# A down projection in Winograd form on one Trainium2 core: the residual added by an accumulating transfer, and quarter sums of w2 kept in device memory

## The chip, the cores and the metric

The kernel runs on one core of one Trainium2 chip. A core has TensorE (PE, matrix products), VectorE (DVE), ScalarE (ACT), GpSimd (POOL) and SyncE (SP, which only issues transfers here). Transfers are issued from the queues of SP, ACT and POOL, and all of them are carried by the core's 16 DMA engines. Times are device microseconds (us) of one execution; the metric is their median over several executions, and lower is better.

## The reference, cut to what matters

One encoder layer is computed for a prompt of 2048 tokens and a sample of 256 tokens, with 1024 channels. The change touches only the end of the layer:

```python
h = rmsnorm(x, norm2_g[i]) * (1.0 + scale2) + shift2          # x is x1, the sum after the mixer
x = x + gate2 * (jnp.square(jax.nn.relu(h @ mlp_w1[i])) @ mlp_w2[i])
...
return rmsnorm(x, final_g)
```

`mlp_w2` is 4096 x 1024. Everything is float32, and a float32 product is made of three products of split operands (high by high, high by low, low by high).

## The kernel before, in words

The last part of the kernel is the down projection (`h @ mlp_w2`, the gate, the residual x1 and the final norm). The 18 token tiles of 128 tokens stand in nine pairs (`PAIRS`); `acc[2*i]` and `acc[2*i+1]` are the two tiles of pair i, each 128 x 1024, and stay in SBUF from the first addition to the output. The 4096 hidden channels are cut into four groups (g = 0 to 3). Each group is a 2 x 2 block product in Winograd form: seven products per pair, numbered o = 1 to 7, each of 12 matmuls of 128 x 512. The left operands come from device memory (`AD`, loaded into `araw`) and are split into high and low parts (`aop`: an ACT cast and a DVE subtraction, line 778). The right operands are quarters of w2, or sums of quarters, loaded by SP into `w2raw` (six buffers, half a quarter of 512 KB each), summed on DVE (lines 1107 and 1109) and split into `w2op` (three buffers).

A group is walked in sweeps over the pairs: (1, 6, 7), (2), (5, 3), (4) for groups 0 to 2, and (2), (1, 6, 7), (5, 3, 4) for group 3. Within a sweep the products are staggered: at step i come the first product of pair i, the second of pair i - 1 and the third of pair i - 2. A sweep of three has 27 products, 324 matmuls. Products of one pair in a sweep can share a PSUM bank and go on accumulating in it, so the second may start only when DVE has added the first into `acc` (line 1202).

The right operands are w2 quarters named by two digits: o = 5 needs 01 - 00, o = 6 needs 11 - (01 - 00), and o = 4 needs 10 - (11 - (01 - 00)). Each of the three starts again from the quarters: `w2_load` fetches two, three and four of them, for each of two halves h.

In group 3, `res(i, h)` applies the gate and adds x1 as soon as a tile has its first five terms, in the sweep (1, 6, 7): POOL multiplies `acc` by the gate `g2` (line 1159), adds `xe` (line 1160, x1 loaded from `X1` into three buffers) and issues the next load of x1 (`res_load`, line 1151). In the last sweep (5, 3, 4) each product is multiplied by the gate into `tm` and added (`last_add`, lines 1174 and 1175), ACT takes the sums of squares, and `out` applies the norm and stores the tile: for eight prompt tiles by ACT and a POOL multiplication (lines 1188 and 1189), for the other ten by one DVE operation (line 1191).

The program is written in the order of the loops; a planner then orders the instructions of each engine by its own estimates of their costs, and each engine and each queue runs its own in that order.

Of the kernel before, what the change touches and what calls it, by code (L numbers as in the profile page):

```python
# [9 lines left out]
F32 = mybir.dt.float32  # L10
# [3 lines left out]
ALU = mybir.AluOpType  # L14
# [4 lines left out]
P = 128  # L19
D = 1024  # L20
KT = 8
T = 16
# [8 lines left out]
PAIRS = ((0, 1), (2, 3), (4, 5), (6, 7), (8, 16), (9, 17), (10, 11), (12, 13), (14, 15))  # L31
# [105 lines left out]
def body(ctx, tc, I, O):  # L137
    nc = tc.nc
    v = nc.vector
    dram = ctx.enter_context(tc.tile_pool(name="dr", bufs=1, space=DRAM))  # L140
# [7 lines left out]
    def ps():  # L148
        return psp[0].tile([P, 512], F32, name="ps", tag="ps")
# [6 lines left out]
    X1 = dram.tile([NTILE, P, D], F32, name="X1")  # L156
    HOP = [dram.tile([3, P, 7, 4, P], F32, name=f"HOP{b}") for b in range(3)]
    WS = dram.tile([16, P, 4, 4, P], F32, name="WS")
    AD = [[dram.tile([P, 7, 4, 384], F32, name=f"AD{g}_{b}") for b in range(3)] for g in range(4)]

    R = "right"
# [267 lines left out]
    for part, (pw, tc_, tb_, t16) in enumerate(((PR, ARc, ARb, AR16), (PI, AIc, AIb, AI16))):  # L429
        for k0 in (0, 4, 8):  # L430
            n = 4 if k0 < 8 else 2
# [94 lines left out]
    for t0 in range(0, T, 4):  # L526
        dg_ = dgn
        for k in range(KT):
# [5 lines left out]
            for _ in range(SQ[t0 // 4] if k >= 4 else 0):  # L534
                t = next(ts, None)
# [22 lines left out]
    for g in range(0, 16, 2):  # L558
        pq = ps()
        for i in range(2):  # L560
            for m in range(2):
                x = 2 * i + m
# [149 lines left out]
    for b4 in range(16):  # L712
        u = load_u(l2, b4, 3)
        for q in range(4):
# [3 lines left out]
            for m in range(2):  # L718
                o = py[:, m * NCH:(m + 1) * NCH]
# [8 lines left out]
    for k in range(KT):  # L728
        for hb in range(2):
# [5 lines left out]
            for q in range(4):  # L735
                g = 4 * b4 + q
                py = ps()
                hf, hb_ = Hs[:, g, :], Hs[:, 64 + g, ::-1]
                for m, (of, ob) in enumerate(((0, 0), (128, 128))):
                    o = py[:, m * NCH:(m + 1) * NCH]  # L740
# [33 lines left out]
    def split(hi, lo, src, chain=False):  # L774
        with ExitStack() as st:
            for x in last if chain else ():
                st.enter_context(tc.issue_after(x.ins))
            ins = (nc.scalar.copy(hi, src), v.tensor_tensor(lo, src, hi.bitcast(F32), op=ALU.subtract))  # L778
        if chain:
            last[:] = ins  # L780
        return ins
# [134 lines left out]
    t = GORD[-1]  # L916
# [26 lines left out]
    def w_ops(b, i):  # L943
        ws = WS[i].rearrange("p o k c -> p (o k) c")
        one, two, both = slice(0, 1), slice(1, 2), slice(0, 2)
        ca, cb = (slice(256 * i + P * x, 256 * i + P * x + P) for x in range(2))
        if b == 0:
            ra, rb = w_raw((both, w1v[:, :, ca])), w_raw((both, w1v[:, :, cb]))
            yield w_split(ra)
            s = w_raw()  # L950
            v.tensor_tensor(s[:, 1], rb[:, 0], rb[:, 1], op=ALU.add)
            v.tensor_tensor(s[:, 0], s[:, 1], ra[:, 0], op=ALU.subtract)
            nc.gpsimd.dma_start(ws[:, 0:8], s.rearrange("p o k c -> p (o k) c"))
            yield w_split(s)
            v.tensor_tensor(rb[:, 0], ra[:, 0], rb[:, 0], op=ALU.subtract)
            v.tensor_tensor(ra[:, 1], ra[:, 1], s[:, 0], op=ALU.subtract)
            nc.gpsimd.dma_start(ws[:, 8:12], rb[:, 0])
            nc.gpsimd.dma_start(ws[:, 12:16], ra[:, 1])
            yield w_split(rb)
            yield w_split(ra[:, two])  # L960
        else:
            yield w_split(w_raw((both, w1v[:, :, ca])))
            yield w_split(w_raw((both, ws[:, 0:8])))
            yield w_split(w_raw((one, ws[:, 8:12]), (two, w1v[:, 4:8, cb])))
            yield w_split(w_raw((one, ws[:, 12:16]))[:, one])
# [12 lines left out]
    def product(bank, lhs, rhs, start):  # L978
        for k in range(4):
            for x, (a, b) in enumerate(((0, 0), (0, 1), (1, 0))):  # L980
                nc.tensor.matmul(bank, lhsT=lhs(a, k), rhs=rhs(b, k), start=start and k == 0 and x == 0,  # L981
                                 stop=k == 3 and x == 2, skip_group_check=True)

    def up_group(b, pairs, hops, load=None):
# [45 lines left out]
        for y in ys:  # L1030
# [10 lines left out]
            i = pairs[y]  # L1041
            nc.gpsimd.dma_start(AD[i // 4][b][:, :, i % 4], c[:, 0:7])  # L1042

# [39 lines left out]
    w2v = I["mlp_w2"].rearrange("o (g k a p) (d m) -> (o g) a d p k m", g=4, k=4, a=2, d=2)  # L1083
# [3 lines left out]

    def w2_load(g, o):

        need = {1: ("00",), 2: ("10",), 3: ("11",), 7: ("01", "11"), 5: ("01", "00"), 6: ("01", "00", "11"),  # L1090
                4: ("01", "00", "11", "10")}[o]
        for h in range(2):
            parts = []
            for a, d in need:
                x = dn.tile([P, 2, 512], F32, name="w2raw", bufs=6)
                nc.sync.dma_start(x, w2v[g, int(a), int(d), :, 2 * h:2 * h + 2])
                parts.append(x)
            yield parts

    def w2_op(g, o, loads=None):  # L1100
        op = None
        for h, (x, *more) in enumerate(loads or w2_load(g, o)):
            if op is None:
                op = dn.tile([P, 2, 4, 512], F32R, name="w2op", bufs=3)
            for n, y in enumerate(more):
                if n == 0 and o != 7:
                    v.tensor_tensor(x, x, y, op=ALU.subtract)  # L1107
                else:
                    v.tensor_tensor(y, y, x, op=ALU.subtract)  # L1109
                    x = y  # L1110
            ks = slice(2 * h, 2 * h + 2)
            late[:] = split(op[:, 0, ks], op[:, 1, ks], x)
        return op
# [3 lines left out]
    def a_op(g, i, o):  # L1117
        raw = dn.tile([P, 4, P], F32, name="araw", bufs=4)
        nc.sync.dma_start(raw, AD[g][i // 3][:, AOP[o], :, P * (i % 3):P * (i % 3) + P])
        op = dn.tile([P, 2, 4, P], F32R, name="aop", bufs=5)  # L1120
        late[:] = split(op[:, 0], op[:, 1], raw)
        return op
# [11 lines left out]
    dr = tc.alloc_tile_pool(name="dr", bufs=1, side=R, reuse_waits="tile")  # L1134
    g2 = dr.tile([P, 2, 2, 512], F32, name="g2")
    fgb = dr.tile([P, D], F32, name="fgb")
    xe = [dr.tile([P, 2, 512], F32, name=f"xe{i}") for i in range(3)]
    tms = [dr.tile([P, 512], F32, name=f"tm{i}") for i in range(2)]
    acc = [dr.tile([P, 2, 512], F32, name=f"acc{i}") for i in range(18)]
    state = {}  # L1140
    nres = [0, 0, 0]
    order = []
    for i in range(9 + 2):
        order += [(i - n, n - 1) for n in (1, 2) if 0 <= i - n < 9]

    def res_load():
        n = nres[2]
        if n < 18:
            nres[2] += 1
            i, h = order[n]  # L1150
            (nc.scalar if n < 3 else nc.gpsimd).dma_start(xe[n % 3].rearrange("p d m -> p (d m)"), X1[PAIRS[i][h]])

    def res(i, h):

        t = PAIRS[i][h]
        x = xe[nres[0] % 3]
        nres[0] += 1
        a = acc[2 * i + h]
        nc.gpsimd.tensor_tensor(a, a, g2[:, 0 if t < T else 1], op=ALU.mult)  # L1159
        nc.gpsimd.tensor_tensor(a, a, x, op=ALU.add)  # L1160
        res_load()

    def sumsq(i, h, d):
        if (i, h) not in state:
            state[i, h] = dr.tile([P, 2], F32, name="ss2", bufs=18)
        nc.scalar.activation(junk[:, 512 * d:512 * d + 512], acc[2 * i + h][:, d], AF.Square,
                             accum_out=state[i, h][:, d:d + 1])

    def last_add(i, h, d, bank):
        r = 0 if PAIRS[i][h] < T else 1  # L1170
        tm = tms[nres[1] % 2]
        nres[1] += 1
        a = acc[2 * i + h][:, d]
        v.tensor_tensor(tm, bank, g2[:, r, d], op=ALU.mult)  # L1174
        v.tensor_tensor(a, a, tm, op=ALU.add)  # L1175
        sumsq(i, h, d)
# [53 lines left out]
    for g in range(4):  # L1230
        for sweep in SW[g]:
            ws = [w2.pop((g, o)) if (g, o) in w2 else w2_op(g, o) for o in sweep]
            if g == 2 and sweep == (4,):
                with tc.issue_after(late[0].ins):
                    for r in range(2):
                        for j in range(2):
                            nc.scalar.dma_start(g2[:, r, j], MODD[10 + j, r:r + 1, :].partition_broadcast(P))
                    nc.scalar.dma_start(fgb, I["final_g"].rearrange("(o d) -> o d", o=1).partition_broadcast(P))
                    for n in range(3):
                        res_load()  # L1240
            banks = {}
            for i in range(9 + len(sweep) - 1):
                for n, o in enumerate(sweep):
                    j = i - n
                    if not 0 <= j < 9:
                        continue
                    op = aops.pop((g, j, o)) if (g, j, o) in aops else a_op(g, j, o)
                    start = o in (1, 2, 5, 4)
                    if start:
                        banks[j] = ps()  # L1250
                    w = ws[n]
                    product(banks[j], lambda a, k: op[:, a, k], lambda a, k: w[:, a, k], start)
                    done(g, o, j, banks[j])
# [32 lines left out]
```

## Time and profile before

| | |
|---|---|
| median of 3 executions | 2529.23 us (2527.2 to 2534.12) |
| the profiled execution | 2526.02 us, of which its span is 2524.2 us |
| mean granted TensorE clock | 0.968 |
| busy share of the span | PE 93%, PEld 80%, DVE 68%, ACT 39%, POOL 10% |
| the down projection | from about 1750 us to the end |

The span runs from the first to the last instruction of the profiled execution. Busy shares are means over stages with different limits, so a stage has to be read by itself.

### The profile page before, as it was taken

What the parts mean: (1) busy time and instruction counts of PE and PEld (TensorE: products, weight loads), DVE (VectorE), ACT (ScalarE), POOL (GpSimd) and SP (SyncE); (2) the same over time, 40 slices, a digit from 0 to 9 for tenths busy, and PEclk for the clock granted to TensorE, in tenths of its full rate; (3) what the DMA queues carried; (4) which work ended last, traced back from release to release, by engine and by line L of the source; (5) the groups of instructions that cost most, each with busy time, mean ns of one, the idle gap of its engine ahead of it and who ended that gap; (6) DMA issues with size and microseconds to landing.
All of it is one profiled execution on the core that took longest, in us unless ns stands there. A gap on an engine that the chain in (4) does not pass through costs nothing. (4 is left out here: it accounts for less than half of the span.)

```text
span 2524.2 us, 33957 instructions
## 1 busy us (share of the span) xinstructions
PE 2342.9 (93%) x12461; PEld 2028.7 (80%) x12461; DVE 1706.2 (68%) x2954; ACT 977.5 (39%) x1805; POOL 256.9 (10%) x269
## 2 busy tenths in 40 slices
PE   5799889987999999799999999998999999999876
PEld 2699448886788888699999999998788888878655
DVE  6776778944444344887776667666476676767998
ACT  3766332233433333533443344333433323333234
POOL 1000000000010010121100000000000000001953
PEclk9999999998999999899999999999999999999988
DMA  9722676688333334787786677676685465666544
GB/s 250 291 96 92 219 230 178 194 332 239 122 113 109 103 119 135 252 262 245 252 269 217 213 258 226 223 229 219 188 255 173 136 215 171 196 218 191 181 136 146
DMA packets 419094, 498.27 MB, mean 197 GB/s; under 512 B 42000, under 2 KB 311584, under 8 KB 416880
## 3 DMA queue, kind: packets, MB, share of 16 engines
q1 hardware_dynamic: 380512, 357.93, 45.5%
q0 software_dynamic: 32448, 124.45, 14.0%
q10 hardware_dynamic: 5968, 13.72, 1.8%
q8 instruction: 98, 1.61, 0.3%
q14 instruction: 68, 0.56, 0.1%
HBM read 339.09 MB, written 156.94 MB: 197 GB/s over the span
## 5 line engine op out<-in xcount | busy, mean ns | idle before, releaser
L981 PE MATMUL ps<-w2op,aop 128*128 128x512 f32 x3024 | 712.1, 398 | 43.7 <-DVE acc L1202 16.3
L981 PEld LDWEIGHTS ps<-w2op,aop 128*128 128x128 f32 x3024 | 579.2, 192 | 176.5 <-issue 26.9
L981 PE MATMUL ps<-hop,wop 128*128 128x384 f32 x4032 | 706.1, 336 | 14.7 <-ACT r L1002 8.7
L981 PEld LDWEIGHTS ps<-hop,wop 128*128 128x128 f32 x4032 | 703.4, 189 | 17.5 <-ACT r L1002 10.0
L778 ACT CAST aop<-araw 128x512 fp32r<-128x512 f32 x252 | 156.3, 622 | 383.9 <-PE ps L981 336.1
L778 ACT CAST wop<-wraw 128x1024 fp32r<-128x1024 f32 x192 | 181.3, 946 | 159.1 <-PE ps L981 139.8
L778 DVE TENSOR_TENSOR aop<-araw,aop 128x512 fp32r<-128x512 f32 x252 | 208.0, 829 | 37.8 <-ACT aop L778 37.8
L1202 DVE TENSOR_TENSOR acc<-ps,acc 128x512 f32<-128x512 f32 (+1 forms) x198 | 150.5, 760 | 110.9 <-PE ps L981 110.9
L778 DVE TENSOR_TENSOR wop<-wraw,wop 128x1024 fp32r<-128x1024 f32 x192 | 207.1, 1086 | 19.2 <-ACT wop L778 18.6
L819 PE MATMUL ps<-wh,gh 128*128 128x512 f32 x552 | 210.8, 398 | 1.5 <-ACT gh L778 1.5
L819 PE MATMUL ps<-wh,gl 128*128 128x512 f32 x552 | 208.3, 393 | 2.1 <-DVE rs_a L119 2.1
L819 PE MATMUL ps<-wl,gh 128*128 128x512 f32 x552 | 206.4, 390 | 0.0
L819 PEld LDWEIGHTS ps<-wh,gl 128*128 128x128 f32 x552 | 104.0, 188 | 26.8 <-DVE gl L778 2.6
L819 PEld LDWEIGHTS ps<-wl,gh 128*128 128x128 f32 x552 | 104.1, 189 | 22.6
L819 PEld LDWEIGHTS ps<-wh,gh 128*128 128x128 f32 x552 | 104.0, 189 | 22.4 <-ACT gh L778 2.0
L1016 DVE TENSOR_TENSOR ct<-ps,r 128x384 f32<-128x384 f32 x48 | 26.6, 557 | 135.6 <-DMA AD<-ct 135.6
L829 DVE TENSOR_TENSOR m<-ps,m 128x256 f32<-128x256 f32 x72 | 29.8, 423 | 127.9 <-ACT m L828 126.4
L1035 DVE SCALAR_TENSOR_TENSOR ct<-ct 128x1152 f32<-128x1152 f32 (+1 forms) x96 | 91.3, 953 | 27.0 <-ACT ct L1032 26.9
L687 PE MATMUL hsb<-Hs,jswp 128*128 128x128 f32 x280 | 92.8, 420 | 15.9 <-DVE Hs L693 12.2
L1042 POOL DMA_DIRECT2D AD<-ct x48 | 45.1, 939 | 577.7 <-DVE ct L1037 383.4
L1159 POOL TENSOR_TENSOR acc<-acc,g 128x1024 f32<-128x1024 f32 x18 | 45.4, 2523 | 568.6 <-DVE acc L1202 568.4
L828 ACT ACTIVATE m<-ps 128x256 f32<-128x256 f32 x72 | 26.7, 386 | 173.0 <-PE ps L819 172.8
(306 smaller groups left out, 3044.6 us busy)
## 6 DMA issues: line engine op xcount, KB each, us to landing
AD<-ct POOLq DMA_DIRECT2D x48, 1344.0 KB, 7.5
araw<-AD SPq DMA_DIRECT2D x252, 256.0 KB, 3.3
w2raw<-in_mlp_w_dram SPq DMA_DIRECT2D x112, 512.0 KB, 4.8
wraw<-in_mlp_w_dram SPq DMA_DIRECT2D x64, 512.0 KB, 4.9
adaw<-in_ada_w_dram SPq DMA_DIRECT2D x48, 512.0 KB, 4.6
CAD<-ca SPq DMA_DIRECT2D x32, 512.0 KB, 3.6
u<-UT SPq DMA_DIRECT2D x64, 256.0 KB, 3.9
ca<-CAD SPq DMA_DIRECT2D x16, 1024.0 KB, 7.0
```

Of the source, the lines that this page charges most:

```text
L687: nc.tensor.matmul(hs, lhsT=jswp, rhs=h, start=True, stop=True)
L778: ins = (nc.scalar.copy(hi, src), v.tensor_tensor(lo, src, hi.bitcast(F32), op=ALU.subtract))
L819: nc.tensor.matmul(banks[q], lhsT=st[:, k if ks is None else ks], rhs=mv[k].rearrange("p (a q m) -> p q a m", a=2, q=4)[:, q], start=first ...
L828: nc.scalar.activation(m[:, sl], banks[q][:, 256:512], AF.Sigmoid)
L829: v.tensor_tensor(m[:, sl], banks[q][:, 0:256], m[:, sl], op=ALU.mult)
L981: nc.tensor.matmul(bank, lhsT=lhs(a, k), rhs=rhs(b, k), start=start and k == 0 and x == 0, stop=k == 3 and x == 2, skip_group_check=True)
L1016: v.tensor_tensor(ct[y][:, 0], bank[y, "w"], r1[y], op=ALU.add)
L1035: v.scalar_tensor_tensor(c[:, x], c[:, x], 0.0, c[:, x], op0=ALU.max, op1=ALU.mult)
L1042: nc.gpsimd.dma_start(AD[i // 4][b][:, :, i % 4], c[:, 0:7])
L1159: nc.gpsimd.tensor_tensor(a, a, g2[:, 0 if t < T else 1], op=ALU.mult)
L1202: v.tensor_tensor(a, bank, a, op=ALU.add)
```

## The change

In `res`, the gate is now applied by DVE, and x1 is added to `acc` by an accumulating transfer from `X1`, issued by POOL; the buffers `xe` and their 18 loads go. In `w2_op`, when the operand of o = 6 is made, its two sums (T1 = 01 - 00 and T2 = 11 - T1) are stored from POOL's queue to a new array `TD` in device memory; the operand of o = 5 is then loaded as T1, and that of o = 4 is 10 - T2.

```diff
+    TD = dram.tile([4, 2, 2, P, 2, 512], F32, name="TD")
...
-        need = {1: ("00",), 2: ("10",), 3: ("11",), 7: ("01", "11"), 5: ("01", "00"), 6: ("01", "00", "11"),
-                4: ("01", "00", "11", "10")}[o]
+        need = {1: ("00",), 2: ("10",), 3: ("11",), 7: ("01", "11"), 5: ("t1",), 6: ("01", "00", "11"),
+                4: ("t2", "10")}[o]
...
-                nc.sync.dma_start(x, w2v[g, int(a), int(d), :, 2 * h:2 * h + 2])
+                src = TD[g, int(q[1]) - 1, h] if q[0] == "t" else w2v[g, int(q[0]), int(q[1]), :, 2 * h:2 * h + 2]
+                nc.sync.dma_start(x, src)
...
-                if n == 0 and o != 7:
+                if o == 6 and n == 0:
                     v.tensor_tensor(x, x, y, op=ALU.subtract)
+                    nc.gpsimd.dma_start(TD[g, 0, h], x)
                 else:
                     v.tensor_tensor(y, y, x, op=ALU.subtract)
                     x = y
+                    if o == 6:
+                        nc.gpsimd.dma_start(TD[g, 1, h], x)
...
     def res(i, h):
         t = PAIRS[i][h]
-        x = xe[nres[0] % 3]
-        nres[0] += 1
         a = acc[2 * i + h]
-        nc.gpsimd.tensor_tensor(a, a, g2[:, 0 if t < T else 1], op=ALU.mult)
-        nc.gpsimd.tensor_tensor(a, a, x, op=ALU.add)
-        res_load()
+        v.tensor_tensor(a, a, g2[:, 0 if t < T else 1], op=ALU.mult)
+        nc.gpsimd.dma_start(a.rearrange("p d m -> p (d m)"), X1[t], accum_op=ALU.add)
```

The function `res_load`, its order of loads and its three calls in the sweep (4) of group 2 are deleted too.

## Rows read from the trace of the kernel before

**Rows 1.** Windows by stage: busy time and instructions by engine, clock, DMA.

```profile
core 0: us, PE busy (x) PEld busy (x) DVE busy (x) ACT busy (x) POOL busy (x), PEclk, DMA share, GB/s
1750.00:1773.00 23.00, 14.86 (x37) 9.83 (x38) 16.87 (x19) 7.57 (x12) 1.87 (x2) 0.66 0.95 320
1773.00:2310.00 537.00, 534.36 (x2341) 440.03 (x2340) 348.97 (x457) 178.80 (x265) 0.00 (x0) 1.00 0.62 192
...
2310.00:2404.10 94.10, 79.78 (x322) 62.98 (x321) 90.50 (x61) 22.89 (x35) 76.77 (x40) 0.92 0.58 185
2404.10:2524.20 120.10, 83.13 (x329) 66.31 (x327) 113.14 (x204) 49.67 (x121) 51.66 (x28) 0.84 0.42 137
```

**Rows 2.** Timeline of PE from 1745 us: start, length, matmuls, idle before.

```profile
1772.42 98.13 PE L981 MATMUL ps<-w2op,aop 128*128 128x512 f32 x420 [1.19 <-ACT aop L778]
...
2233.62 119.99 PE L981 MATMUL ps<-w2op,aop 128*128 128x512 f32 x528 [1.69 <-DVE acc L1202]
...
2391.68 4.81 PE L981 MATMUL ps<-w2op,aop 128*128 128x512 f32 x12 [5.32 <-DVE acc L1202]
2400.51 10.91 PE L981 MATMUL ps<-w2op,aop 128*128 128x512 f32 x36 [4.02 <-DVE acc L1202]
...
2430.46 59.82 PE L981 MATMUL ps<-w2op,aop 128*128 128x512 f32 x250 [6.54 <-DVE aop L778]
2493.95 10.05 PE L981 MATMUL ps<-w2op,aop 128*128 128x512 f32 x36 [3.67 <-DVE ss L1182]
```

**Rows 3.** POOL's groups from 2250 us to the end: busy, mean ns, idle before.

```profile
L1160 POOL TENSOR_TENSOR acc<-acc,xe 128x1024 f32<-128x1024 f32 x18 | 50.7, 2816 | 1.3
L1159 POOL TENSOR_TENSOR acc<-acc,g 128x1024 f32<-128x1024 f32 x18 | 45.4, 2523 | 568.6 <-DVE acc L1202 568.4
L1189 POOL TENSOR_TENSOR acc<-acc,fgb 128x1024 f32<-128x1024 f32 x8 | 19.1, 2384 | 60.8 <-ACT acc L1188 42.8 <-ACT rs_s L120 18.0
```

**Rows 4.** DVE's groups by form, 1770 to 2300 us.

```profile
L778 DVE TENSOR_TENSOR aop<-araw,aop 128x512 fp32r<-128x512 f32 x196 | 134.4, 688 | 37.8 <-ACT aop L778 37.8
...
L778 DVE TENSOR_TENSOR w2op<-w2raw,w2op 128x1024 fp32r<-128x1024 f32 x44 | 52.8, 1221 | 4.0 <-ACT w2op L778 4.0
```

**Rows 5.** DVE's groups by form, 2310 to 2404.1 us, sweep (1, 6, 7) of group 3.

```profile
L778 DVE TENSOR_TENSOR aop<-araw,aop 128x512 fp32r<-128x512 f32 x25 | 49.8, 1996 | 0.0
L778 DVE TENSOR_TENSOR w2op<-w2raw,w2op 128x1024 fp32r<-128x1024 f32 x5 | 13.0, 2622 | 0.4 <-ACT w2op L778 0.4
L1202 DVE TENSOR_TENSOR acc<-ps,acc 128x512 f32<-128x512 f32 x19 | 12.9, 680 | 1.6 <-PE ps L981 1.6
L1109 DVE TENSOR_TENSOR w2raw<-w2raw 128x1024 f32<-128x1024 f32 x3 | 9.2, 3062 | 0.3 <-DMA w2raw<-in_mlp_w_dram 0.3
...
L1107 DVE TENSOR_TENSOR w2raw<-w2raw 128x1024 f32<-128x1024 f32 x2 | 3.5, 1744 | 2.6 <-DMA w2raw<-in_mlp_w_dram 2.6
```

**Rows 6.** DVE's groups by form, 2404.1 us to the end.

```profile
L1175 DVE TENSOR_TENSOR acc<-acc,tm 128x512 f32<-128x512 f32 x27 | 31.3, 1158 | 0.1
L778 DVE TENSOR_TENSOR aop<-araw,aop 128x512 fp32r<-128x512 f32 x25 | 19.9, 805 | 0.0
...
L778 DVE TENSOR_TENSOR w2op<-w2raw,w2op 128x1024 fp32r<-128x1024 f32 x4 | 13.8, 3459 | 0.0
```

**Rows 7.** Timeline of DVE: around the start of group 0, and at 2430 us.

```profile
1757.62 1.23 DVE L1109 TENSOR_TENSOR w2raw<-w2raw 128x1024 f32<-128x1024 f32 x1
...
1774.40 1.23 DVE L778 TENSOR_TENSOR w2op<-w2raw,w2op 128x1024 fp32r<-128x1024 f32 x1
...
2430.32 2.85 DVE L1175 TENSOR_TENSOR acc<-acc,tm 128x512 f32<-128x512 f32 x1
...
2434.30 0.68 DVE L1175 TENSOR_TENSOR acc<-acc,tm 128x512 f32<-128x512 f32 x1
```

**Rows 8.** DMA from 2310 to 2405 us: packets, MB, share; issues, KB, us to landing.

```profile
q1 hardware_dynamic: 15859, 10.99, 37.5%
q0 software_dynamic: 1833, 6.72, 21.0%
...
xe<-X POOLq DMA_DIRECT2D x13, 512.0 KB, 4.0
```

**Rows 9.** DMA issues of the whole span, from the page: two kinds of POOL stores.

```profile
X<-xg POOLq DMA_DIRECT2D x18, 512.0 KB, 2.9
...
WS<-wraw POOLq DMA_DIRECT2D x16, 512.0 KB, 7.0
```

More of the change, by code (lines that the diff above doesn't have):

```diff
@@ L1088, in w2_load @@
     def w2_load(g, o):
-        need = {1: ("00",), 2: ("10",), 3: ("11",), 7: ("01", "11"), 5: ("01", "00"), 6: ("01", "00", "11"),
-                4: ("01", "00", "11", "10")}[o]
+        need = {1: ("00",), 2: ("10",), 3: ("11",), 7: ("01", "11"), 5: ("t1",), 6: ("01", "00", "11"),
+                4: ("t2", "10")}[o]
         for h in range(2):
             parts = []
-            for a, d in need:
+            for q in need:
                 x = dn.tile([P, 2, 512], F32, name="w2raw", bufs=6)
-                nc.sync.dma_start(x, w2v[g, int(a), int(d), :, 2 * h:2 * h + 2])
+                src = TD[g, int(q[1]) - 1, h] if q[0] == "t" else w2v[g, int(q[0]), int(q[1]), :, 2 * h:2 * h + 2]
+                nc.sync.dma_start(x, src)
                 parts.append(x)
@@ L1136, in body @@
     fgb = dr.tile([P, D], F32, name="fgb")
-    xe = [dr.tile([P, 2, 512], F32, name=f"xe{i}") for i in range(3)]
     tms = [dr.tile([P, 512], F32, name=f"tm{i}") for i in range(2)]
@@ L1140, in body @@
     state = {}
[L1141 to L1151, printed above, removed]
+    nres = [0]
     def res(i, h):
         t = PAIRS[i][h]
-        x = xe[nres[0] % 3]
-        nres[0] += 1
         a = acc[2 * i + h]
-        nc.gpsimd.tensor_tensor(a, a, g2[:, 0 if t < T else 1], op=ALU.mult)
-        nc.gpsimd.tensor_tensor(a, a, x, op=ALU.add)
-        res_load()
+        v.tensor_tensor(a, a, g2[:, 0 if t < T else 1], op=ALU.mult)
+        nc.gpsimd.dma_start(a.rearrange("p d m -> p (d m)"), X1[t], accum_op=ALU.add)
     def sumsq(i, h, d):
@@ L1170, in last_add @@
         r = 0 if PAIRS[i][h] < T else 1
-        tm = tms[nres[1] % 2]
-        nres[1] += 1
+        tm = tms[nres[0] % 2]
+        nres[0] += 1
         a = acc[2 * i + h][:, d]
@@ L1238, in body @@
                     nc.scalar.dma_start(fgb, I["final_g"].rearrange("(o d) -> o d", o=1).partition_broadcast(P))
-                    for n in range(3):
-                        res_load()
             banks = {}
```

## The prediction

> **What bounds the kernel now.** I read the windows by stage first. From 1773 to 2310 us, groups 0 to 2 and the first sweep of group 3, PE is busy 534.4 of 537.0 us at a granted clock of 1.00, which is 2.4 GHz [rows 1]: work saved on DVE there buys nothing. What is left to win lies at the start of the down projection (1750 to 1773 us, PE busy 14.9 of 23) and in the last two sweeps. Their borders come from the timeline of PE: 528 matmuls without a break take 119.99 us, 0.2273 us each, so a sweep of 324 takes 73.6 us at full clock [rows 2]. Counted back from the last matmul, 36, 250, two rows between of 2 and 12, and 24 of the 36 from 2400.51 make 324: the sweep (5, 3, 4) begins at 2404.1 us. In the same way (1, 6, 7) begins at 2310.0 us. The first lasts 94.1 us, and from the second's start to the end it is 120.1 us [rows 1]; PE's own work is 73.6 us in each.
>
> In these two stages DVE is the engine that is always busy: 90.5 of 94.1 and 113.1 of 120.1 us [rows 1]. PE waits for DVE's additions out of PSUM (5.32 and 4.02 us in two of the rows) and for its operand splits (6.54 us) [rows 2]. But the groups by form show that DVE has not so much more to do; it is held up. The 128x512 operand split takes 688 ns and the 128x1024 one 1221 ns before [rows 4]; in the sweep (1, 6, 7) they take 1996 and 2622 ns, and the w2 sums 3062 and 1744 ns, while the addition that reads PSUM takes 680 ns as ever [rows 5]. POOL is busy 76.8 us of that stage, with the 36 operations of `res` (2523 and 2816 ns each) [rows 1, 3]. Each DVE operation with two SBUF inputs that meets one of them stands until it ends. When the last has gone the same line falls from 2.85 to 0.68 us [rows 7]. The stage is bound by DVE waiting for POOL.
>
> **Part 1: the gate on DVE, x1 by transfer.** In (1, 6, 7), take from DVE's 90.5 us what the blocking adds: 25 splits x 1.31 = 32.7, 5 w2 splits x 1.40 = 7.0, 3 sums x 1.84 = 5.5, 2 sums x 0.52 = 1.0 [rows 4, 5], together 46.2; 44.3 us of work stays. Onto it come 18 multiplications of 128x1024 at 1.22, the duration of the other two-input operation of that shape [rows 4]: 22.0. In place of it, part 2 takes out four sums (4.9), and some work that today slips behind 2404.1 comes back into the stage (two more 128x1024 additions and up to three w2 splits, 2.4 to 6.1). DVE then has 64 to 68 us in a stage where PE needs 73.6: PE would set the pace. The bounds are 73.6, and 84.6 if half the multiplications (11 us) come just when a bank or an operand is awaited and nothing catches it up. I take 75, near the lower end, because from 1773 us on PE lost next to nothing beside a DVE busy 349 of 537 us [rows 1], though here DVE is nearer to its limit. The stage gains 94.1 - 75 = 19 us.
>
> In (5, 3, 4) the start is freed as well: four w2 splits there are 13.8 - 4.9 = 8.9 us too long, the aop splits 19.9 - 17.2 = 2.7, and line 1175 is 31.3 - 27 x 0.688 = 12.7 too long [rows 6]. Of this last I give the change 4, two operations of the kind at 2430.32 [rows 7]; the rest is the doing of the eight POOL multiplications by `fgb` (2384 ns each) [rows 3], which stay. That frees 15.6 us, at least 11.6, at most 24.3. Some of the w2 splits are then done before the sweep begins: 0 to 4.9 us, I take 4. So 120.1 - 15.6 - 4 = 100; the bounds are 95 and 104. It stays above PE's 73.6 plus the tail because DVE still has three operations for each product, the norms and eight blockings. Gain 20 us, in all 39.
>
> **The transfers.** Before, nothing accumulates in flight, so the price is bounded from below by the plain load of x1: 18 loads of 512 KB, on the software queue at 21.0% of 95 us for 6.72 MB, 1.56 us of all 16 engines each, 4.0 us to landing [rows 8]. With the other queue's 37.5% [rows 8] the stage needs some 36 + 28 = 64 us of DMA time in 75: it fits. From above I take twice the plain price, for an accumulation has to read its destination too: 3.1 us each, 92 us in 75. Even so the queue of the operands keeps moving, and the accumulations only spill into the next sweep, where DMA is busy 42% [rows 1]. A tile has a whole sweep between its gate and its `last_add`, so I put nothing in the sum; if this cover goes, it is the first rival. On POOL nothing is queued behind them but one another and the late output operations. The 18 loads into `xe` and their issue time go with the waits on three buffers.
>
> The Trainium skill (Collectives: The Full Stack, "The bandwidth ceiling: the fold count and why AG ≠ RS ≠ AR") says that a reduction in a transfer is slower not because of the addition but because of its two source reads, and measures about half the rate of a copy. No row here shows it. By the page, an estimate is the twofold price above, which my sum bears; one at a time, it is the rival below.
>
> **Part 2: sums kept in device memory.** Per group four DVE sums for o = 4 and two for o = 5 go, and six loads of 512 KB for four stores. In groups 0 to 2 PE covers the saving whole [rows 1]. The stores add a wait: a `w2raw` buffer with T1 or T2 comes free when its store has landed, not when DVE has read it. Behind the waiting load on SP's queue stand the `araw` loads, for those ACT's casts, for those PE. Also, the loads of T1 and T2 wait for their stores, a sweep or more earlier. In steady state operands lie in six buffers well ahead, and I take nothing. At the start there is no such lead. DVE's second sum is read at 1757.62, the operand of o = 7 is ready at 1775.6 [rows 7], and PE, unbroken from 1772.42 at 98.13 / 420 = 0.234 us a matmul, wants it some 24 matmuls later, at 1778.0 [rows 2]: 2.4 us to spare. A 512 KB store from POOL lands 2.9 to 7.0 us after its issue [rows 9], and four of them are 2.1 MB in a stage in which DMA is busy 95% at 320 GB/s [rows 1], 6.5 us if they all come first. So 0 to 11 us; I take 3, since most of the stores come after the loads that matter.
>
> **The sum.** -19 - 20 + 3 = -36 us. The profiled execution took 2526.0 us, 1.8 more than its span, and would take 2490. It lay 3.2 us under the median, so against the median 2529.2 - 36 = 2493 us.
>
> **The rivals.**
> 1. *The accumulations are late (the other side).* If they run one at a time at c us, the last of 18 lands 18 c after the first issue. This is about 2321 (four products into the stage), and the last tile is wanted some 22 products (60 us) after 2385: 124 us, so c = 6.9 is free. Every DVE split stands behind a waiting `last_add`. At the 8.0 of two plain landings [rows 8] it costs 20 us: 2513. Above c = 8.9 nothing of the gain is left, above 9.3 the kernel is more than 0.3% (7.6 us, about what a measurement here can tell from none) slower. For it speaks that nothing is known of c; against it that plain loads of one queue overlap. By the page's rule above this is the case to fear, if transfers do not overlap. Chance 0.10, half of it slower.
> 2. *DVE becomes the bound in (1, 6, 7) after all*, its burst of w2 splits and gates out of step with PE: 84.6 and 104 instead of 75 and 100 gives 14 us less: 2507. For it speaks that DVE has 64 to 68 us in 73.6. Chance 0.13.
> 3. *The buffers held by the stores stall PE*, at the start (11 instead of 3: 2501) or also once a group by a landing of 7.0 us (2522). Against it: 349 of 537 us of DVE and no stall show that operands are early. Chance 0.08.
> 4. *The change doesn't do what it says*: POOL is not what stretches DVE, and the gates are only added, 22 + 3 us: 2554. Against it stand the unchanged PSUM reads and the fall to 0.68 us. Chance 0.02.
> 5. *Everything meets its lower bound and more*: 73.6, 95 and nothing lost at the start give 2484, and each us by which the last sweep comes below 95 is one less; for that the eight remaining blockings would have to hurt less than today. Chance of under 2483: 0.04.
>
> **How the numbers follow.** The forecast has 0.63, with a range of its own of 2483 to 2505: from 73.6, 95 and 0 to 80, 104 and 5. For 8 in 10 I reach to 2480 and to 2511, which takes in rival 2, the short form of rival 3 and a little of rivals 1 and 5. Slower holds half of rival 1, rival 4 and some of it for what I have not seen: 0.07; no change 0.03; faster 0.90.
>
> **What would show it.** Right: in (1, 6, 7) the aop split is back at about 0.69 us, POOL is idle but for its issues, PE is busy over 95% at full clock, and that sweep takes about 75 us; in (5, 3, 4) the only long DVE operations are eight, beside the multiplications by `fgb`. Wrong: a `last_add` or a sum of squares that waits for a DMA into `acc` (rival 1); PE waiting for DVE's additions at normal DVE durations (rival 2); SP waiting for a store into `TD`, or PE idle more than 10 us between 1750 and 1785 (rival 3); the splits still at 2 us with POOL idle (rival 4).

## The result, and the profile after

The changed kernel takes 2499.07 us (median of 4; 2496.7 to 2501.2) against 2529.67 us before it on the same chip (median of 4): 0.9877 of the time before, with an interval of 0.986 to 0.9894. That is 30.6 us less, where 36 were forecast; 2493 us was predicted and 2480 to 2511 given as the range. A second set (experiment e11) gave 2497.7 us and the same ratio.

The profiled execution took 2500.3 us, its span 2498.5. The windows of the changed kernel are set at its own stages: the start of the down projection, groups 0 to 2 with the first sweep of group 3, the sweep (1, 6, 7), and the rest.

```profile
core 0: us, PE busy (x) PEld busy (x) DVE busy (x) ACT busy (x) POOL busy (x), PEclk, DMA share, GB/s
1753.00:1780.00 27.00, 12.83 (x37) 8.33 (x37) 16.97 (x19) 7.30 (x11) 4.03 (x6) 0.72 0.94 325
1780.00:2314.60 534.60, 533.57 (x2341) 440.70 (x2342) 327.90 (x437) 179.10 (x265) 6.40 (x12) 1.00 0.60 184
2314.60:2392.00 77.40, 74.33 (x323) 61.17 (x322) 62.08 (x74) 23.03 (x35) 13.83 (x16) 0.98 0.92 212
2392.00:2498.50 106.50, 80.69 (x327) 65.09 (x326) 94.66 (x204) 49.79 (x121) 26.14 (x18) 0.87 0.53 160
```

Against [rows 1], the sweep (1, 6, 7) went from 94.1 to 77.4 us, with DVE busy 62.1 instead of 90.5 us although it now does the gates, and POOL 13.8 instead of 76.8. The rest went from 120.1 to 106.5 us. DMA is the figure that rose, from 0.58 to 0.92 in the sweep.

The groups of DVE by form, first in the sweep (1, 6, 7), then in the last stage, show what became of the stretched operations of [rows 5, 6]:

```profile
L1151 DVE TENSOR_TENSOR acc<-acc,g 128x1024 f32<-128x1024 f32 x16 | 19.5, 1220 | 0.0
L779 DVE TENSOR_TENSOR aop<-araw,aop 128x512 fp32r<-128x512 f32 x24 | 16.4, 686 | 6.9 <-ACT aop L779 6.9
...
L779 DVE TENSOR_TENSOR w2op<-w2raw,w2op 128x1024 fp32r<-128x1024 f32 x5 | 5.9, 1221 | 0.6 <-ACT w2op L779 0.6
L1112 DVE TENSOR_TENSOR w2raw<-w2raw 128x1024 f32<-128x1024 f32 x2 | 2.5, 1226 | 6.1 <-DMA w2raw<-in_mlp_w_dram 6.1
```

```profile
L1166 DVE TENSOR_TENSOR acc<-acc,tm 128x512 f32<-128x512 f32 x27 | 22.7, 841 | 0.1
...
L123 DVE SCALAR_TENSOR_TENSOR rs_s<-rs_y,rs_a 128x1 f32<-128x1 f32 x18 | 14.5, 808 | 0.2
...
L779 DVE TENSOR_TENSOR w2op<-w2raw,w2op 128x1024 fp32r<-128x1024 f32 x3 | 3.5, 1218 | 0.0
...
L1151 DVE TENSOR_TENSOR acc<-acc,g 128x1024 f32<-128x1024 f32 x2 | 2.4, 1216 | 0.0
```

The operand split fell from 1996 to 686 ns, the w2 split from 2622 to 1221, and the gate costs the 1.22 us it was priced at. In the last stage two kinds are still long in the mean, the addition (841 ns) and an operation of one column, `rs_s` (808 ns): POOL's eight multiplications by `fgb` are still there, and exactly eight DVE operations of this stage are stretched, two additions (2.8 us each) and six `rs_s` (1.7 to 2.2 us). Three w2 splits and two gates lie behind the border, so DVE entered the last sweep with work left over.

The timeline of PE shows the three places where it still waits: at the start, at the border of the last two sweeps, and near the end.

```profile
1772.03 2.50 PE L982 MATMUL ps<-w2op,aop 128*128 128x512 f32 x5 [0.76 <-DVE w2op L779]
1779.94 114.25 PE L982 MATMUL ps<-w2op,aop 128*128 128x512 f32 x492 [5.41 <-ACT aop L779]
...
2388.49 8.21 PE L982 MATMUL ps<-w2op,aop 128*128 128x512 f32 x28 [3.08 <-DVE acc L1193]
2400.65 64.70 PE L982 MATMUL ps<-w2op,aop 128*128 128x512 f32 x272 [3.96 <-DVE tm L1165]
2468.52 11.29 PE L982 MATMUL ps<-w2op,aop 128*128 128x512 f32 x36 [3.17 <-DVE ss L1173]
```

The first of these waits is the one that the stores to `TD` make. SP's queue, POOL's, and what SP waited for, all at the start:

```profile
1731.01 41.08 SPq L1098 DMA_DIRECT2D w2raw<-in_mlp_w_dram  x10
1772.14 4.05 SPq L1124 DMA_DIRECT2D araw<-AD  x4
```

```profile
1761.02 0.55 POOL L1110 DMA_DIRECT2D TD<-w2raw  x1 [4.03 <-DVE w2raw L1109]
1762.28 0.54 POOL L1115 DMA_DIRECT2D TD<-w2raw  x1 [0.70 <-DVE w2raw L1112]
```

```profile
SPq L1098 <- DMA TD<-w2raw: 9.6, 2, 9.2
```

SP issued its w2 loads from 1731.0 to 1772.1 us, because buffers came free only when the stores issued at 1761.0 and 1762.3 had landed (9.2 us of waiting in one piece), and only then the next four `araw` loads. ACT's cast waits for those and PE for the cast, 5.41 us. The late w2 load itself holds up almost as long: ACT stood 6.24 us at a cast of w2 whose sum on DVE waited for that load, and was through 0.8 us before the `araw` tile came.

Of the two waits at the border, the first, 3.08 us, lies 12 matmuls ahead of it. The addition for which PE waits stands in DVE's order behind a w2 sum, and DVE stood at that sum for a load, which SP issued at 2377.4 us, when a split begun on DVE at 2376.2 had freed one of the six buffers:

```profile
2385.39 1.23 DVE L1112 TENSOR_TENSOR w2raw<-w2raw 128x1024 f32<-128x1024 f32 x1 [3.37 <-DMA w2raw<-in_mlp_w_dram]
```

The second, 3.96 us, is of another kind. Before the first operation of the last sweep for which PE waits (`tm`), DVE had the left-over gates and w2 splits to do, at their usual durations:

```profile
2394.24 2.35 DVE L1151 TENSOR_TENSOR acc<-acc,g 128x1024 f32<-128x1024 f32 x2
2396.51 3.49 DVE L779 TENSOR_TENSOR w2op<-w2raw,w2op 128x1024 fp32r<-128x1024 f32 x3
```

The DMA of the sweep (1, 6, 7), to set against [rows 8]:

```profile
q0 software_dynamic: 2105, 7.71, 54.1%
q1 hardware_dynamic: 13988, 8.63, 37.2%
...
acc<-X POOLq DMA_DIRECT2D x16, 512.0 KB, 7.0
araw<-AD SPq DMA_DIRECT2D x24, 256.0 KB, 7.0
```

54.1% of 77.4 us for 7.71 MB is 2.85 us of all 16 engines for an accumulation of 512 KB, against 1.56 for the plain load [rows 8]: 1.8 times. It lands after 7.0 us instead of 4.0. The `araw` loads beside it also take 7.0 us.

For the comparisons below the stages were counted matmul by matmul in each profiled execution: the start (first to 37th matmul of the down projection), then up to the sweep (1, 6, 7) of group 3, this sweep, and the rest of the span. By this count the sweeps of before last 95.9 and 118.5 us; the border is at 2405.8 us, 1.7 later than the prediction's even division of one row gave.

| kernel | start | to (1, 6, 7) | (1, 6, 7) | rest | median us | ratio to before, interval |
|---|---|---|---|---|---|---|
| before | 21.6 | 537.5 | 95.9 | 118.5 | 2529.7 | |
| changed | 25.9 | 534.6 | 78.4 | 105.6 | 2499.1 | 0.9877 (0.986 to 0.9894) |
| e1 residual alone | 21.5 | 536.8 | 81.7 | 108.0 | 2504.3 | 0.9894 (0.9874 to 0.9914) |
| e2 sums alone | 26.3 | 539.8 | 93.3 | 120.0 | 2537.1 | 1.0038 (1.0024 to 1.0051) |
| e3 spare POOL work | 26.4 | 583.6 | 75.4 | 105.0 | 2546.7 | 1.0072 (1.0059 to 1.0085) |
| e4 plain load elsewhere | 33.2 | 537.3 | 73.4 | 104.9 | 2503.7 | 0.9899 (0.9886 to 0.9912) |
| e5 no sums in group 0 | 21.6 | 538.9 | 75.5 | 105.1 | 2496.8 | 0.9869 (0.9851 to 0.9887) |
| e6 = e5, output on DVE | 21.5 | 538.6 | 77.1 | 94.7 | 2486.2 | 0.9831 (0.981 to 0.9852) |
| e7 = e5, plain load | 21.4 | 540.5 | 74.0 | 105.3 | 2498.2 | 0.9878 (0.9863 to 0.9892) |
| e8 nine buffers, output on DVE | 20.5 | 550.5 | 73.4 | 93.5 | 2493.5 | 0.9863 (0.9847 to 0.988) |
| e9 = e1, output on DVE | 21.6 | 536.6 | 78.2 | 96.9 | 2492.1 | 0.9857 (0.9833 to 0.988) |
| e10 residual all on DVE | 26.2 | 540.6 | 84.2 | 109.3 | 2514.9 | 0.9947 (0.9929 to 0.9965) |
| e11 changed, again | 26.1 | 534.4 | 78.9 | 105.7 | 2497.7 | 0.9877 (0.9856 to 0.9899) |

What lies ahead of the first of these matmuls is the same program in all of them, and varies from 1749.7 to 1760.3 us between the profiled executions; so stages tell more than spans. The changed kernel's stages repeat within 0.5 us (e11). Between e1 and e9, and between e5 and e6, the edits differ only in `out`, and DVE's order is the same up to 2440 us; yet their sweeps (1, 6, 7) differ by 3.5 and 1.6 us. A difference of 1 to 3 us in that sweep between two kernels, each profiled once, therefore cannot be told from none.

### The profile page after: what moved, and what is told of

Its sections match the earlier page's. It is cut to its first block, busy times and chain, and to the rows that moved or that the text cites. A ratio compares the mean times of both kernels' runs of the same rounds, so it can differ in the third digit from the quotient of the medians.

```text
span 2498.5 us, 33896 instructions
## 1 busy us (share of the span) xinstructions
PE 2335.6 (93%) x12461; PEld 2027.3 (81%) x12461; DVE 1638.7 (66%) x2948; ACT 978.8 (39%) x1805; POOL 177.1 (7%) x252
## 4 chain that ended last, share of the span: by engine, by line
PE 68%; issue 13%; DVE 10%; DMA 5%; ACT 2%; POOL 1%; SPq 1%; ACTq 0%; POOLq 0%; DVEq 0%
PE ps L982 46%; PE ps L820 10%; PE ps L627 2%; PE hsb L688 2%; PE pa L277 1%; DVE Hs L694 1%; DVE c L691 1%; DMA hraw<-HOP 1%; DVE c L692 1%; DMA ca<-CAD 1%; PE pc L652 1%; DMA w2raw<-in_mlp_w_dram 1%; PE ps L615 1%; DVE c L693 1%; PE ps L511 1%
## 5 line engine op out<-in xcount | busy, mean ns | idle before, releaser
L982 PE MATMUL ps<-w2op,aop 128*128 128x512 f32 x3024 | 701.4, 394 | 27.0 <-ACT aop L779 8.1
L779 DVE TENSOR_TENSOR wop<-wraw,wop 128x1024 fp32r<-128x1024 f32 x192 | 207.0, 1087 | 18.4 <-ACT wop L779 17.8
L779 DVE TENSOR_TENSOR aop<-araw,aop 128x512 fp32r<-128x512 f32 x252 | 172.4, 688 | 52.5 <-ACT aop L779 52.5
L1003 ACT COPY r<-ps 128x384 f32<-128x384 f32 x96 | 45.9, 480 | 114.2 <-PE ps L982 114.2
```

The source lines that it names most:

```text
L1003: nc.scalar.copy(r[y], bank[y, name])
```

## The experiments

**e1 and e2: the two parts alone.** e1 takes from the diff only `res` and the deletion of `res_load`; e2 takes only `TD`, `w2_load` and `w2_op`.

> The residual part alone: gate on DVE and accumulating transfer, no sums kept in device memory (w2 operands made from quarters as before). Theory (nearly all of the gain comes from POOL no longer blocking DVE, and the stores cost the start 4.4 us): the start of group 0 is back at 21.6 us between the first matmul and unbroken PE, the sweep (1, 6, 7) of group 3 stays within 76 to 82 us, total 2493 to 2503. Rival (the kept sums bring half of the gain): 2512 to 2518.

> The kept sums alone: residual on POOL as before. Theory: start of group 0 loses some 4 us as in the changed kernel, and the four sums saved in the last group give 5 to 10 us back while DVE is still blocked: 2522 to 2532 in all, no clear change. Rival (the kept sums bring half of the gain): 2512 to 2518.

e1 keeps most of the gain, 25.0 us: 2504.3 us, ratio 0.9894, (1, 6, 7) at 81.7 us, the start at 21.5. The median is a little above the theory's 2503 and far from the rival's. e2 is slower than before, by 0.24 to 0.51%, which neither had expected: 2537.1 us, 5 above the theory. Its start lost 4.7 us as foreseen, but the saved sums gave back only 2.6 in (1, 6, 7), and the rest did not fall at all. The windows of e2 in its last two stages, and the operand split in the first of them, show why: POOL is as busy as before, and so DVE's time goes in blocking, not in sums.

```profile
2322.50:2415.80 93.30, 79.16 (x326) 63.04 (x325) 87.47 (x59) 22.89 (x35) 77.23 (x40) 0.93 0.53 169
2415.80:2535.80 120.00, 79.83 (x325) 62.87 (x323) 109.60 (x202) 49.73 (x121) 50.98 (x28) 0.85 0.41 134
```

```profile
L779 DVE TENSOR_TENSOR aop<-araw,aop 128x512 fp32r<-128x512 f32 x25 | 52.2, 2093 | 3.0 <-ACT aop L779 3.0
```

The two parts do not add up: 25.0 us gained and 7.8 lost, each alone, are 17, and together they gain 30.6. By the stages, e2's loss beyond the start lies partly in groups 0 to 2 (see e10); no run takes the rest apart.

**e3: POOL busy with nothing.**

```diff
         nc.gpsimd.dma_start(a.rearrange("p d m -> p (d m)"), X1[t], accum_op=ALU.add)
+        for _ in range(2):
+            nc.gpsimd.tensor_tensor(pj, pj, g2[:, 0], op=ALU.mult)
```

> The changed kernel, and behind each accumulating transfer two POOL multiplications of 128x1024 on a tile of their own that nothing else reads or writes. Theory (POOL operations with two SBUF inputs block DVE by themselves): the operand split in the sweep (1, 6, 7) is back at about 2 us, that sweep at 90 to 96 us, total 2518 to 2535. Rival (the gain came from the waits on xe and acc that went, or from a new order of DVE): 2496 to 2503, splits at 0.69 us.

2546.7 us, 47.6 more than the changed kernel and above the theory's 2535. Nothing depends on the added work, so the planner ordered it earlier than `res`, right after the load of `g2`: it ran in group 2 and the first sweep of group 3, and it is there that the time was lost (583.6 us instead of 534.6), while (1, 6, 7) stayed short. The place of the prediction was wrong and its cause right. DVE and POOL in e3, from 2119.5 to 2365.6 us and from 2050 us to the end:

```profile
L779 DVE TENSOR_TENSOR aop<-araw,aop 128x512 fp32r<-128x512 f32 x72 | 83.1, 1155 | 0.8 <-ACT aop L779 0.8
L1197 DVE TENSOR_TENSOR acc<-ps,acc 128x512 f32<-128x512 f32 x63 | 43.1, 684 | 31.7 <-PE ps L982 31.7
```

```profile
L1156 POOL TENSOR_TENSOR pj<-pj,g 128x1024 f32<-128x1024 f32 x36 | 98.3, 2731 | 171.5 <-DMA g<-MODD 168.8
```

A stretch of the kernel in which PE had been unbroken [rows 1] loses 49 us to 36 POOL operations that share no written tile with anything. Additions that read PSUM stay at 684 ns, splits from SBUF go to 1155 in the mean. No data dependence and no changed order is needed for the loss: in the down projection DVE's 730 operations come in the same order as in the changed kernel.

**e4 and e7: what the accumulation costs.** e4 loads x1 into spare tiles, so that x1 is left out of the result; e7 is e5 (below) with `accum_op` taken away, so that x1 overwrites the sums.

```diff
-        nc.gpsimd.dma_start(a.rearrange("p d m -> p (d m)"), X1[t], accum_op=ALU.add)
+        x = pj[(2 * i + h) % 3]
+        nc.gpsimd.dma_start(x.rearrange("p d m -> p (d m)"), X1[t])
```

> The changed kernel with the accumulating transfer made a plain load of the same 512 KB into one of three spare tiles, so that x1 is left out of the result. Theory (an accumulation takes the DMA engines about twice the time of a plain load, and this delays operands): DMA share in (1, 6, 7) falls from 0.92 to about 0.7, the sweep from 77.4 to 74 or 75 us, PE loses less at the border of the sweeps, total 2492 to 2497. Rival (DMA is hidden; the 3.8 us over PE's time are DVE's): 2498 to 2501.

> The kernel of e5 with the 18 accumulating transfers made plain loads into the same tiles at the same places, so that the sums in them are overwritten by x1 and the result is not the reference's. Theory (an accumulation costs the DMA engines about twice a plain load, and operands come late for it): packets of the software queue at about 190 ns instead of 355, the sweep (1, 6, 7) at 74 to 75.5 us instead of 78, total 3 to 5 us below e5. Rival (only the presence of the transfers or DVE's load makes the 4 us): same as e5 within 2 us.

e4 didn't test what it was made for. Nothing tied the spare loads to the gates, and POOL issued them at the start of the down projection, the first at 1761 us. In (1, 6, 7) there was then no x1 traffic at all, and this sweep fell to 73.4 us, PE's own time; but the start, where DMA is already full, took 33.2 us instead of 25.9. The total (2503.7 us) fits neither expectation. The windows of e4 at the start and in (1, 6, 7):

```profile
1753.00:1787.00 34.00, 13.36 (x37) 8.69 (x38) 17.27 (x19) 6.83 (x10) 8.67 (x15) 0.62 0.98 357
...
2324.10:2397.50 73.40, 73.40 (x325) 60.81 (x324) 62.53 (x74) 23.14 (x35) 0.00 (x0) 1.00 0.41 119
```

e7 keeps the places and the waits. The DMA of its sweep (1, 6, 7):

```profile
q0 software_dynamic: 2159, 7.87, 33.9%
...
acc<-X POOLq DMA_DIRECT2D x16, 512.0 KB, 4.5
araw<-AD SPq DMA_DIRECT2D x24, 256.0 KB, 4.4
```

33.9% of 74.1 us for 7.87 MB is 1.67 us for each plain load in this place, so an accumulation's 2.85 is 1.7 times that. The sweep is 74.0 us, 1.5 less than in e5, which by itself is within what kernels vary there; but DVE's wait for the last w2 load of the sweep is shorter too: 0.6 us here, none in e4, and 1.3 to 3.9 in the seven kernels that accumulate with six buffers. But the total doesn't follow: 2498.2 against 2496.8 us. Theory on the engines' time, rival on the whole: the price exists, and the stage after it takes as long with or without it (105.3 and 105.1 us).

**e5: no sums in group 0.**

```diff
+        if g == 0:
+            need = {5: ("01", "00"), 4: ("01", "00", "11", "10")}.get(o, need)
...
-                if o == 6 and n == 0:
+                if n == 0 and (o == 6 or g == 0 and o != 7):
                     v.tensor_tensor(x, x, y, op=ALU.subtract)
-                    nc.gpsimd.dma_start(TD[g, 0, h], x)
+                    if g:
+                        nc.gpsimd.dma_start(TD[g, 0, h], x)
```

(and the store of T2 likewise only for g above 0)

> The changed kernel, but group 0 makes its operands from the quarters as before and stores no sums; groups 1 to 3 are unchanged. Theory (the stores of group 0 hold buffers for which SP waits): the start of group 0 is back at about 21.6 us instead of 25.9, the stages of group 3 stay at 78 and 106 us, total 4 us below the changed kernel: 2493 to 2497. Rival (the start is slow for another reason, as the transfers' common load): 2498 to 2501.

The start is back at 21.6 us, so it is the stores that make that wait (whether by the buffers that they hold or by their bytes, e8 tells). The total is 2496.8 us, within the theory's range, but the intervals of e5 and of the changed kernel (0.9851 to 0.9887 and 0.986 to 0.9894) overlap nearly whole, and the stages say that little was won: what the start gains, the next stage gives back (538.9 instead of 534.6). The timeline of PE in e5 has two waits at the borders of group 0's sweeps, 3.0 us together, where the changed kernel has one of 0.40:

```profile
1881.57 16.59 PE L982 MATMUL ps<-w2op,aop 128*128 128x512 f32 x72 [1.43 <-DVE acc L1196]
1899.73 338.05 PE L982 MATMUL ps<-w2op,aop 128*128 128x512 f32 x1488 [1.57 <-DVE acc L1196]
```

Start and next stage together are 560.5 us in the changed kernel, in e5 and in e11, 559.0 before and 558.3 in e1: in these kernels keeping the sums costs about 2 us up to the last group, wherever it is begun. In e2 and e10, which also load `xe`, it is 566.1 and 566.7 (see e10).

**e6, e8 and e9: the rest of POOL's work.** In `out`, `pool = False`: all 18 tiles are finished by the one DVE operation that ten of them had already. e6 adds it to e5, e9 to e1, and e8 to the changed kernel with `bufs=9` for `w2raw`.

> The kernel of e5 with all 18 output tiles scaled and multiplied by DVE in one operation each, none by ACT and POOL. Theory (each POOL multiplication still blocks a DVE operation for some 2 us, more than the 1.28 us that it saves DVE): the last stage falls by 5 to 8 us against e5, total 2486 to 2491. Rival (DVE has no room for eight more operations in the last sweep): same as e5 or some us more, 2493 to 2503.

> The changed kernel with nine w2raw buffers instead of six (in the space of the removed xe) and all output tiles on DVE, as in e6; all groups keep their sums. Theory (the start loses by the held buffers, not by the bytes of the stores): the start is at 21 to 23 us, total as e6: 2486 to 2492. Rival (2.1 MB of stores in a stage with DMA at 95% cost by themselves): the start at 25 to 27 us and the total some 4 us above e6.

> The residual part alone (e1) with all output tiles on DVE (as in e6): no sums are kept in device memory in any group. Theory (outside group 3 PE covers the saving; in group 3 four sums fewer on DVE and six loads fewer are worth 2 to 5 us): (1, 6, 7) at 77 to 82 us, total 2486 to 2492, level with e6 or some us above. Rival (the kept sums matter beyond that): over 2495.

e6 is the fastest: 2486.2 us, ratio 0.9831, and its interval ends (0.9852) where e5's begins (0.9851); its slowest execution (2491.9 us) is faster than e5's fastest (2493.9). The last stage of e5, then of e6, in windows and in the two lines that change their length:

```profile
2396.30:2501.40 105.10, 76.43 (x325) 61.94 (x323) 94.88 (x205) 49.58 (x121) 26.53 (x19) 0.88 0.54 163
```

```profile
L1169 DVE TENSOR_TENSOR acc<-acc,tm 128x512 f32<-128x512 f32 x27 | 22.7, 842 | 0.1
...
L123 DVE SCALAR_TENSOR_TENSOR rs_s<-rs_y,rs_a 128x1 f32<-128x1 f32 x18 | 14.5, 808 | 0.2
```

```profile
2391.20:2485.90 94.70, 77.00 (x325) 61.55 (x323) 86.73 (x212) 41.36 (x113) 1.72 (x2) 0.93 0.59 178
```

```profile
L1169 DVE TENSOR_TENSOR acc<-acc,tm 128x512 f32<-128x512 f32 x27 | 18.5, 684 | 0.0
...
L123 DVE SCALAR_TENSOR_TENSOR rs_s<-rs_y,rs_a 128x1 f32<-128x1 f32 x18 | 3.9, 214 | 0.1
```

DVE has eight operations of 1.28 us more and is busy 8.2 us less; on the two lines the eight POOL multiplications had cost it 14.8 us, 1.9 each. The stage fell by 10.4 us, more than the 5 to 8 of the theory, and 7.8 of it lie behind the last matmul (21.4 us in e5, 13.6 in e6). e8 shows the same in its rest (93.5 us) and the shortest start of all (20.5), so the buffers and not the bytes of the stores made the wait. Its sweep (1, 6, 7) shows more: with all the accumulations and a DMA share of 0.91 it takes PE's own time, at full clock.

```profile
2324.00:2397.40 73.40, 73.40 (x325) 60.82 (x324) 61.78 (x74) 23.15 (x35) 13.75 (x16) 1.00 0.91 198
```

With nine buffers SP issued the last w2 load at 2307.7 us, before this sweep began, and DVE did not wait for one in it. But e8 lost some 12 us in the long stage, and its total, 2493.5 us, is 1.5 above the theory's range. PE waited at four borders of sweeps for an addition of DVE, two of them here, from the timeline of PE in e8, with DVE's longest wait ahead of the first.

```profile
1876.42 173.13 PE L982 MATMUL ps<-w2op,aop 128*128 128x512 f32 x756 [3.42 <-DVE acc L1193]
2053.88 173.14 PE L982 MATMUL ps<-w2op,aop 128*128 128x512 f32 x756 [4.32 <-DVE acc L1193]
```

```profile
1865.05 1.22 DVE L1112 TENSOR_TENSOR w2raw<-w2raw 128x1024 f32<-128x1024 f32 x1 [6.18 <-DMA w2raw<-in_mlp_w_dram]
```

It is the pattern of 2385.39 above: DVE stands at a w2 sum whose load has not landed, and the additions for which PE waits stand behind it in DVE's order. In that stage DVE's waits for w2 loads sum to 37.2 us, against 34.8 in the changed kernel, so it is their place more than their sum that differs; DVE's order differs from the changed kernel's from about 1806 us on. No run tries nine buffers in the changed kernel's order.

e9, without any kept sums, comes to 2492.1 us, the edge of the theory's range; its interval (0.9833 to 0.988) overlaps e6's. The kept sums are worth 1 us in (1, 6, 7) and 2 in the rest against e6, less the 2 they cost earlier: too little to be told from none.

**e10: both operations on DVE.** The loads into `xe` stay; in `res` of before only the engine is changed, with the kept sums as in the changed kernel.

```diff
-        nc.gpsimd.tensor_tensor(a, a, g2[:, 0 if t < T else 1], op=ALU.mult)
-        nc.gpsimd.tensor_tensor(a, a, x, op=ALU.add)
+        v.tensor_tensor(a, a, g2[:, 0 if t < T else 1], op=ALU.mult)
+        v.tensor_tensor(a, a, x, op=ALU.add)
```

> The changed kernel, but x1 is loaded into xe as before and both operations of the residual are done by DVE, with no accumulating transfer and no POOL operation in them. Theory (the gain is POOL's silence; the accumulating transfer only spares DVE 22 us of additions): DVE gets 62 + 22 = 84 us in the sweep (1, 6, 7) and becomes its bound, 84 to 90 us, the total 2505 to 2513. Rival (the transfers' price eats what they spare): 2496 to 2502.

2514.9 us, with (1, 6, 7) at 84.2 us, as the theory had it, and the total 2 us above its range. Its windows there:

```profile
2319.90:2404.10 84.20, 77.34 (x325) 62.09 (x324) 78.86 (x89) 22.52 (x34) 7.94 (x15) 0.97 0.60 188
```

DVE is busy 78.9 of 84.2 us. So moving all of `res` off POOL gives about half of the gain, and the accumulating transfer in place of loads into `xe` and additions on DVE, for all its DMA time, the other half: 17 us against e11, measured beside it. By the stages only 8.9 of these lie in the last two; 6.2 lie in the stage before, where no `res` runs yet. In group 2 PE waits there 4.16 us for an addition of DVE, behind a w2 sum whose load was issued at 2230.5 us, right after the first three loads into `xe` (2225.6 to 2229.6). e2, with the same loads, waits 3.87 us at the same matmul, before 1.69, and e11 less than 0.25. That these loads are the cause is not shown by a run of its own.

**e11: the changed kernel again.**

> The changed kernel once more, beside the two others of this call, as their base: 2496 to 2502, start of group 0 at 25 to 27 us, (1, 6, 7) at 76 to 79 us.

As expected: 2497.7 us.

## Why the prediction was right, and where it was off

*What bound the stages* was read rightly: DVE held by POOL. e3 shows it without any data in common, and in the changed kernel the splits are at 686 ns, as was said they would be.

*The sweep (1, 6, 7)* was put at 75 us, from 94.1; it took 77.4 by the same division. DVE was priced at 64 to 68 us and was busy 62.1. PE sets the pace, as forecast. Of the 3.8 us over PE's 73.6, 3.08 are the one wait of PE behind the late w2 load. The accumulations' traffic very likely has a part in it, since DVE hardly waits for that load when x1 goes elsewhere (e4, 73.4 us) or is plain (e7, 74.0). But it is not a price of the traffic by itself: e8 has it whole and takes 73.4 us, with its last w2 load issued before the sweep. The prediction let the transfers spill and did not look for a load that six buffers hold back until the end of the sweep.

*The last stage* is the term that was mis-sized: 100 us forecast, with bounds of 95 and 104, and 106.5 measured, above its bounds. The freed blocking was sized about rightly: DVE's busy time fell from 113.1 to 94.7 us, 18.4, where 15.6 were put down (a w2 sum of 3.4 us in this stage had been left out). But the forecast took each of these us off the stage, and 4 more because w2 splits would be done before the border; only one of the four was, with two gates and a wide addition behind it too. DVE's idle time, taken as the 7.0 us of before, rose to 11.8: the table of waits has 6.3 us in which DVE waited for others in this stage (2.0 for ACT's operand casts, 2.4 for PE), against 1.9 before. Counted from the rows of PE, by the division of the table of stages, 118.5 us before were 73.6 for the matmuls at full clock, 16.8 of waits over 0.25 us, 20.2 behind the last matmul, and 7.9 left for slower matmuls and small gaps; in the changed kernel the 105.6 are 73.6, 7.1, 18.7 and 6.2. (The granted clock of the two stages is 0.84 and 0.87.) So nearly all of the gain came out of PE's waits, and the tail, in which PE has nothing left to do, fell by only 1.5 us; it is 13.6 us in e6, without the eight POOL multiplications. The forecast had made no such split, so its 6.5 us cannot be divided further; that they aren't the accumulations' DMA time, e7 shows.

*The start* was put at 3 us out of 0 to 11. It lost 4.4 us by the chain described (store, buffer, SP's queue, `araw`, cast, PE), with the late w2 load as a second branch of nearly the same length, and the next stage took 2.9 less than before: about 1.5 net. How far these 2.9 are the loss caught up is not shown; e1, which loses nothing at the start, has 0.7 of them.

*The transfers* were put at nothing in the sum, with a price between the plain one and twice that. The Trainium skill (Collectives: The Full Stack, "The bandwidth ceiling: the fold count and why AG ≠ RS ≠ AR") measures about half the rate of a copy for a reduce-scatter in a ring of cores, and gives its two source reads as the reason; carried over to a transfer into SBUF, which that section does not measure, twice the time is an estimate. Here it was 1.7 to 1.8 times in the engines' time, so the trace agrees nearly. The first rival fell all the same: 18 accumulations, of which the 16 in (1, 6, 7) land after 7.0 us in the median and 8.4 at most, held up no `last_add`, and one ACT sum of squares for 5.8 us, early in (1, 6, 7), where ACT is busy 23 of 77 us. The cover named for them, a whole sweep, held.

*The sum* was -36 and came to -30.6 between the medians. Between the profiled executions the terms are -16.7, -13.6 and +1.5 instead of -19, -20 and +3, together -28.8. These executions differ by only 25.7 us, because ahead of the first matmul of the down projection the profiled execution of before was 3.1 us early, as its 3.2 us under the median had told.

*Rivals 2 and 3* each had a small share of the truth, and signs named for them showed. PE waited 3.08 and 3.96 us for DVE at normal durations; the second is rival 2's burst of gates and w2 splits, at the border, and the first is not, since DVE itself stood waiting. SP waited 9.6 us for stores into `TD`, and between 1750 and 1785 us PE is idle 15.8 us (8.1 before); the net price was 1.5 us. Rival 4 is refuted by e3.

## What to carry to other kernels

When an engine is busy all of a stage, compare the mean duration of its operations with that of the same form elsewhere: a stage that looked full of DVE work here was half blocking, and taking POOL's two-input operations away was worth more than the 22 us of work that DVE took over. Do not stop at the operations that one meant to move: the eight that were left cost DVE 1.9 us each, and taking them to DVE as well gave another 10 us (e6). A saving in a stage that another engine covers buys nothing, and a store put beside it to make the saving possible can cost: look for the queue that stands behind the buffer it holds, and for the engine that stands in order before a late load (e8).

## What was not expected of the hardware

POOL's multiplication held up even a DVE operation of one column: `rs_s` took 808 ns in the mean with the eight multiplications beside it and 214 without. An accumulating transfer into SBUF also costs POOL more to issue. POOL's groups in the last two stages of the changed kernel:

```profile
L1152 POOL DMA_DIRECT2D acc<-X x18 | 15.5, 864 | 107.3 <-PE ps L982 60.5 <-DVE acc L1151 43.9 <-issue 2.9
L1184 POOL DMA_DIRECT2D out_y_prompt_dram<-acc x8 | 4.6, 579 | 2.9 <-POOL acc L1180 2.9
```

864 ns each, where a plain store of the same tile takes 579 and the plain load in e7 529, and 18 of them take POOL 15.5 us; this costs nothing here, since DVE's operations beside them keep their usual length.
